# Time-step projection of a decoder trunk: normed x as the standing operand, 16 weight columns as the moving one

## The chip, the core and the metric

The kernel runs on one core of one Trainium2 chip. The metric is the device time of one execution in microseconds (us), the median of several runs. In all that follows PE is TensorE, PEld its weight loads (the loading of the operand that stands in the array), ACT is ScalarE, DVE is VectorE, POOL is GpSimd, and SP is the engine whose queue issues the DMAs.

## What is computed

The reference is one step of a two-layer decoder trunk over 1024 prompt tokens and 8 sample tokens. The change touches layer 0 alone, in the Mamba-2 part, where a raw time step for each of 16 heads is projected out of the normed x:

```
hn = _rmsnorm(x, norm_even[k])
proj = jnp.einsum('bld,de->ble', hn, w_in_even[k])
z, xbc, dt_raw, u, v, g = jnp.split(proj, EVEN_SPLITS, axis=-1)
...
dt = jax.nn.softplus(dt_raw.astype(jnp.float32) + dt_bias.astype(jnp.float32))
a = -jnp.exp(a_log.astype(jnp.float32))
...
da = jnp.transpose((dt * a).reshape(bsz, nc, T, G, E), (0, 1, 3, 4, 2))
cs = jnp.cumsum(da, axis=-1)
```

`dt_raw` has 16 of the 5648 columns of the projection. All other columns, the scan, the gates, the layer 1 and the outputs are the same in both kernels.

## The kernel before

The 1032 tokens (`NT`) lie along the free axis in nearly all of the kernel, and 128 features on the partitions. `hnh` and `hnl` hold the normed x as a high and a low part in float32r, 8 blocks (`k`) of 128 features by 1032 tokens. `unit` computes 128 output columns: it loads a weight block, splits it into high and low (`wh` by ACT at line 103, `wl` by DVE at line 104), and for each of three chunks of 344 tokens runs 8 blocks of three matmuls (lines 115 to 117): weights stand, x passes.

At the start, x comes in tokens on the partitions. For each of nine token blocks, `x_norm` norms a block, PE turns it (tiles `xnT`, line 220, two groups of four transposes, one in the bank pair `sA` and one in `sB`), ACT casts a group to `hnh` (line 223), and DVE takes the rest to `hnl` (line 224), which frees the bank. Each of `sA` and `sB` has two banks, so the second group of block 8 can be written when DVE has done the second group of block 6. While that goes on, PE works on the first two units, `B0` and `C0` (`mm_B`, `mm_C`), chunk by chunk as the tokens come, and on transposes of the parameters (`pct`, line 284).

`dt_unit` (line 376 of the kernel before) then makes the time steps. It loads 16 weight columns and splits them into a tile `wh_dt` of 128 x 8 x 32 (16 high columns beside 16 low ones), runs 3 chunks x 8 blocks x 2 matmuls with these columns standing and 344 tokens passing (lines 388 and 389), and ACT copies the 32 x 1032 result to `draw` (line 390). Ten small matmuls against a selecting matrix `sel` (lines 397 and 400) turn it to tokens on the partitions and add the two halves. Then DVE and ACT run `softplus` on 128 x 144 values, `dA` is formed with `ea` (the exponential of `ear`, 16 values loaded to all partitions by a DMA of its own, line 394), and PE makes the running sums (`cs`, `csT`, lines 408 to 419), which go to DRAM for the scan of the heads.

Every engine works its queue in order. The order is set at build time by a scheduler that walks the program with priorities (earlier in the program text goes first among what it takes to be ready), so that a statement that stands earlier in the text can land earlier in an engine's queue. A tile of a pool waits for the readers of the buffer's former tile; `ear` and `draw` are of the pool tag `mt` that also held the normed blocks `xn`. All DMAs are issued by SP in one queue.

Of the kernel before, what the change touches and what calls it, by code (L numbers as in the profile page):

```python
# [8 lines left out]
F32 = mybir.dt.float32  # L9
# [4 lines left out]
P = 128  # L14
L = 1024
NS = 8
NT = L + NS
CH = NT // 3
NB = 8
# [25 lines left out]
def tile_trunk(ctx, tc, a, o):  # L45
    nc = tc.nc
    V, S, T, G, SY = nc.vector, nc.scalar, nc.tensor, nc.gpsimd, nc.sync

    cp = ctx.enter_context(tc.tile_pool(name="cp", bufs=1))
# [6 lines left out]
    def blk(tag, name, shape=None, dt=F32):  # L56
        return hp.tile(shape or [P, NT], dt, name=name, tag=tag, bufs=NTAG[tag])

    def bank(tag, name):
        return pp.tile([P, 512], F32, name=name, tag=tag, bufs=4 if tag == "mm" else 2)  # L60
# [7 lines left out]
    def rowb(src, off, n, parts=P):  # L68
        return bass.AP(tensor=src.tensor, offset=src.offset + off, ap=[[0, parts], [1, n]])

    def tok(c):
        return (P, c * P) if c < 8 else (NS, L)

    ident = cp.tile([P, P], F32, name="ident")
# [16 lines left out]
    hn = [(hnh[:, k, :], hnl[:, k, :]) for k in range(NB)]  # L91
# [97 lines left out]
    for c in range(9):  # L189
        n = P if c < 8 else NS  # L190
# [161 lines left out]
    csv = cp.tile([P, 128], F32, name="csv")  # L352
    dec = cp.tile([P, 128], F32, name="dec")
    dtot = cp.tile([P, 128], F32, name="dtot")
    sel = cp.tile([32, 16], F32, name="sel")
    dtb = cp.tile([P, 16], F32, name="dtb")
    ea = cp.tile([P, 16], F32, name="ea")
    csd = dram("csd", [8, 16, P])
# [1 line left out]
    def softplus(dst, t, n, name):  # L360
        tm = blk("ld", "spt_" + name, [P, 4, n])
        e, s, s2, p = (tm[:, i, :] for i in range(4))
        V.scalar_tensor_tensor(e, t, -1.0, t, op0=OP.mult, op1=OP.max)
        S.activation(e, e, AF.Exp, scale=-1.0)
        V.tensor_scalar(s, e, 2.0, None, op0=OP.add)
        V.reciprocal(s, s)
        V.tensor_mul(s, s, e)
        V.tensor_mul(s2, s, s)
        V.tensor_scalar(p, s2, 1.0 / 15.0, None, op0=OP.mult)
        for q in (13.0, 11.0, 9.0, 7.0, 5.0, 3.0):  # L370
            V.scalar_tensor_tensor(p, p, 1.0 / q, s2, op0=OP.add, op1=OP.mult)
        V.scalar_tensor_tensor(p, p, 1.0, s, op0=OP.add, op1=OP.mult)
        V.tensor_scalar(e, t, 0.0, None, op0=OP.max)
        V.scalar_tensor_tensor(dst, p, 2.0, e, op0=OP.mult, op1=OP.add)

    def dt_unit():
        draw = blk("mt", "draw", [32, NT])
        with tc.high_priority(WPRI):
            raw = wp.tile([P, NB, 16], F32, name="wr_dt", tag="wr")
            SY.dma_start(raw, w_in_e[:, DTC:DTC + 16].rearrange("(k p) c -> p k c", p=P))  # L380
            whl = wp.tile([P, NB, 32], F32R, name="wh_dt", tag="wh")
            S.copy(whl[:, :, :16], raw)
            V.tensor_sub(whl[:, :, 16:], raw, whl[:, :, :16].bitcast(F32))
        for c in range(3):
            ps = bank("mm", f"mm_dt{c}")
            cs = slice(c * CH, (c + 1) * CH)
            for k, (xh, xl) in enumerate(hn):
                T.matmul(ps[:32, :CH], whl[:, k, :], xh[:, cs], start=k == 0, stop=False)
                T.matmul(ps[:16, :CH], whl[:, k, :16], xl[:, cs], start=False, stop=k == NB - 1)
            S.copy(draw[:, cs], ps[:32, :CH])  # L390
        V.tensor_add(sel, ident[:32, :16], ident[:32, 16:32])
        SY.dma_start(dtb, rowb(a["ssd_dt_bias"], 0, 16))
        ear = blk("mt", "ear", [P, 16])
        SY.dma_start(ear, rowb(a["ssd_a_log"], 0, 16))
        S.activation(ea, ear, AF.Exp)
        ps = bank("sA", "dtT")
        T.matmul(ps[:, 128:144], draw[:, :P], sel, start=True, stop=True)
        for c in range(9):
            n, lo = tok(c)
            T.matmul(ps[:n, c * 16:(c + 1) * 16], draw[:, lo:lo + n], sel, start=True, stop=True)  # L400
        dtr = blk("ld", "dtr", [P, 144])
        V.tensor_add(dtr.rearrange("p (c h) -> p c h", h=16), ps[:, :144].rearrange("p (c h) -> p c h", h=16),
                     dtb[:, None, :].to_broadcast([P, 9, 16]))
        softplus(dt, dtr, 144, "dt")
        V.scalar_tensor_tensor(dA.rearrange("p (c h) -> p c h", h=16), dt[:, :128].rearrange("p (c h) -> p c h", h=16),
                               -1.0, ea[:, None, :].to_broadcast([P, 8, 16]), op0=OP.mult, op1=OP.mult)
        ps = bank("sA", "cs")
        T.matmul(ps[:, :128], tri, dA, start=True, stop=True)
        T.matmul(ps[:, 128:256], ones, dA, start=True, stop=True)
        V.tensor_copy(csv, ps[:, :128])  # L410
        V.tensor_sub(dec, ps[:, 128:256], csv)
        S.activation(dec, dec, AF.Exp)
        S.activation(dtot, ps[:, 128:256], AF.Exp)
        csT = blk("ld", "csT", [16, 8, P])
        for q in range(2):
            ps = bank("sA", f"csT{q}")
            for i in range(4):
                c = q * 4 + i
                T.matmul(ps[:16, i * P:(i + 1) * P], dA[:, c * 16:(c + 1) * 16], tri, start=True, stop=True)
            S.copy(csT[:, q * 4:q * 4 + 4, :], ps[:16].rearrange("p (i t) -> p i t", i=4))  # L420
        SY.dma_start(csd.rearrange("c h l -> h c l"), csT)
# [205 lines left out]
    def g_unit(g, u, vl):  # L627
# [14 lines left out]
        SY.dma_start(mbd[g], u)  # L642

    dt_unit()
    for j in range(4):
        xj(j)
# [435 lines left out]
```

## Time and profile before

| | |
|---|---|
| median of 3 runs | 1498.07 us (1497.86 to 1498.74) |
| the profiled execution's own time | 1496.82 us |
| its span, first to last instruction | 1495.1 us |
| mean granted TensorE clock | 0.998 |
| busy: PE, PEld, DVE, ACT | 99%, 96%, 72%, 49% |
| DMA | 161.5 MB, 108 GB/s over the span |

Busy shares are over the whole span. Matmuls overlap in the records, each one's duration reaching over the start of the next, so the pace of a run of matmuls is read from one start to the next, not from the durations.

### The profile page before, as it was taken

The numbers are of one execution on the slowest core, as the hardware profiler recorded it, in microseconds if no ns is written. First come the engines' busy times: TensorE is split into PE (matmuls) and PEld (weight loads), VectorE is DVE, ScalarE is ACT, GpSimd is POOL, SyncE is SP. The second block draws the span as 40 slices with busy tenths as digits, with TensorE's granted clock in tenths as the row PEclk, the third lists the DMA queues.
The fourth block names the chain that finished last, engine by engine and source line by source line (L and its number), as shares of the span: only waits on it lengthen the run. The fifth ranks groups of instructions, "written<-read, shape, count | busy, mean of one in ns | idle before, by whom it ended". The sixth has DMA issues, their size and how long they took to land.

```text
span 1495.1 us, 23709 instructions
## 1 busy us (share of the span) xinstructions
PE 1476.4 (99%) x9850; PEld 1441.9 (96%) x9850; DVE 1077.1 (72%) x1493; ACT 727.0 (49%) x1094; POOL 0.9 (0%) x7
## 2 busy tenths in 40 slices
PE   7999999999999999999999999999999999999997
PEld 6899999999999999999999999999999999999997
DVE  6525676577777873663346799999999999869624
ACT  6457667585753242630224455465546663234313
POOL 0000000000000000000000000000000000000000
PEclk9999999999999999999999999999999999999999
DMA  6225322233325661236432113222222114357502
GB/s 202 71 74 146 110 85 83 61 124 114 102 96 176 213 198 43 91 120 215 141 113 95 51 33 104 75 61 68 64 76 61 43 58 128 100 188 236 158 29 114
DMA packets 179746, 161.52 MB, mean 108 GB/s; under 512 B 11176, under 2 KB 159324, under 8 KB 179606
## 3 DMA queue, kind: packets, MB, share of 16 engines
q1 hardware_dynamic: 179638, 160.01, 34.1%
q8 instruction: 77, 1.26, 0.4%
q14 instruction: 31, 0.25, 0.1%
HBM read 118.91 MB, written 42.18 MB: 108 GB/s over the span
## 4 chain that ended last, share of the span: by engine, by line
PE 91%; DVE 5%; ACT 2%; issue 1%; DMA 0%; SPq 0%; ACTq 0%; DVEq 0%
PE mm_x L115 2%; PE mm_x L117 2%; PE mm_gc L115 2%; PE mm_oa L115 2%; PE mm_ob L115 2%; PE mm_x L116 2%; PE mm_oa L117 2%; PE mm_oa L116 2%; PE mm_u L115 2%; PE mm_g L115 2%; PE mm_ob L117 2%; PE mm_gc L117 2%; PE mm_ob L116 2%; PE mm_u L117 2%; PE mm_g L116 2%; PE mm_g L117 2%
## 5 line engine op out<-in xcount | busy, mean ns | idle before, releaser
L894 DVE SCALAR_TENSOR_TENSOR c<-gl,pc,c 128x1023 f32<-128x1023 f32 (+25 forms) x240 | 294.9, 1260 | 1.1
L115 PE MATMUL mm_xd<-hnh,wh_xd 128*128 128x344 f32 x192 | 62.1, 323 | 0.7 <-ACT wh_xd L103 0.7
L115 PE MATMUL mm_u<-hnh,wh_u 128*128 128x344 f32 x192 | 62.7, 326 | 0.0
L117 PE MATMUL mm_v<-hnh,wl_v 128*128 128x344 f32 x192 | 62.4, 325 | 0.0
L116 PE MATMUL mm_v<-hnl,wh_v 128*128 128x344 f32 x192 | 62.3, 325 | 0.0
L115 PE MATMUL mm_ga<-hnh,wh_ga 128*128 128x344 f32 x192 | 62.2, 324 | 0.0
L115 PE MATMUL mm_v<-hnh,wh_v 128*128 128x344 f32 x192 | 62.2, 324 | 0.0
L117 PE MATMUL mm_x<-hnh,wl_x 128*128 128x344 f32 x192 | 62.1, 324 | 0.0
L117 PE MATMUL mm_gd<-hnh,wl_gd 128*128 128x344 f32 x192 | 62.0, 323 | 0.0
L115 PE MATMUL mm_gd<-hnh,wh_gd 128*128 128x344 f32 x192 | 62.0, 323 | 0.0
L115 PE MATMUL mm_z<-hnh,wh_z 128*128 128x344 f32 x192 | 61.6, 321 | 0.2 <-ACT sz L131 0.2
L115 PE MATMUL mm_x<-hnh,wh_x 128*128 128x344 f32 x192 | 61.8, 322 | 0.0
L116 PE MATMUL mm_u<-hnl,wh_u 128*128 128x344 f32 x192 | 61.7, 321 | 0.0
L115 PE MATMUL mm_g<-hnh,wh_g 128*128 128x344 f32 x192 | 61.7, 321 | 0.0
L116 PE MATMUL mm_g<-hnl,wh_g 128*128 128x344 f32 x192 | 61.7, 321 | 0.0
L116 PE MATMUL mm_x<-hnl,wh_x 128*128 128x344 f32 x192 | 61.7, 321 | 0.0
L115 PE MATMUL mm_gc<-hnh,wh_gc 128*128 128x344 f32 x192 | 61.6, 321 | 0.0
L117 PE MATMUL mm_u<-hnh,wl_u 128*128 128x344 f32 x192 | 61.6, 321 | 0.0
L115 PE MATMUL mm_gb<-hnh,wh_gb 128*128 128x344 f32 x192 | 61.5, 320 | 0.0
L117 PE MATMUL mm_g<-hnh,wl_g 128*128 128x344 f32 x192 | 61.4, 320 | 0.0
L116 PE MATMUL mm_gc<-hnl,wh_gc 128*128 128x344 f32 x192 | 61.4, 320 | 0.0
L116 PE MATMUL mm_gb<-hnl,wh_gb 128*128 128x344 f32 x192 | 61.4, 320 | 0.0
(477 smaller groups left out, 4927.8 us busy)
## 6 DMA issues: line engine op xcount, KB each, us to landing
x<-res SPq DMA_DIRECT2D x16, 516.0 KB
csb<-csd SPq DMA_DIRECT2D x16, 512.0 KB
mbd<-u SPq DMA_DIRECT2D x8, 516.0 KB
mbl<-mbd SPq DMA_DIRECT2D x8, 516.0 KB
rb<-res SPq DMA_DIRECT2D x8, 516.0 KB
res<-rb SPq DMA_DIRECT2D x8, 516.0 KB
res<-x SPq DMA_DIRECT2D x8, 516.0 KB
mdd<-hv SPq DMA_DIRECT2D x8, 516.0 KB
```

The costliest lines, as they stand in the source:

```text
L115: T.matmul(out, wh[:, k, :], xh[:, cs], start=i == 0, stop=False)
L116: T.matmul(out, wh[:, k, :], xl[:, cs], start=False, stop=False)
L117: T.matmul(out, wl[:, k, :], xh[:, cs], start=False, stop=i == NB - 1)
L894: V.scalar_tensor_tensor(c[:, d:L], gl[:, :L - d], w(k), c[:, d:L], op0=OP.mult, op1=OP.add)
```

## The change

The normed x now stands in the array, 128 tokens at a time, and the weight columns pass: for each of 9 token blocks (8 of 128 tokens and one of 8) 8 blocks of features x 2 matmuls, one that passes the 32 columns of `wh_dt` and one that passes 16, all into one bank `mm_dt`, 32 columns for each token block. The result has tokens on the partitions at once, so `draw`, its three copies, `sel` and the ten small matmuls go. DVE adds the bias and the second half in four operations rather than one. In the program text the DMAs of `dtb` and `ear` and the exponential of `ear` now stand ahead of the matmuls rather than behind them; `softplus` and all behind it are unchanged.

```diff
-    sel = cp.tile([32, 16], F32, name="sel")
...
     def dt_unit():
-        draw = blk("mt", "draw", [32, NT])
         with tc.high_priority(WPRI):
             raw = wp.tile([P, NB, 16], F32, name="wr_dt", tag="wr")
             SY.dma_start(raw, w_in_e[:, DTC:DTC + 16].rearrange("(k p) c -> p k c", p=P))
             whl = wp.tile([P, NB, 32], F32R, name="wh_dt", tag="wh")
             S.copy(whl[:, :, :16], raw)
             V.tensor_sub(whl[:, :, 16:], raw, whl[:, :, :16].bitcast(F32))
-        for c in range(3):
-            ps = bank("mm", f"mm_dt{c}")
-            cs = slice(c * CH, (c + 1) * CH)
-            for k, (xh, xl) in enumerate(hn):
-                T.matmul(ps[:32, :CH], whl[:, k, :], xh[:, cs], start=k == 0, stop=False)
-                T.matmul(ps[:16, :CH], whl[:, k, :16], xl[:, cs], start=False, stop=k == NB - 1)
-            S.copy(draw[:, cs], ps[:32, :CH])
-        V.tensor_add(sel, ident[:32, :16], ident[:32, 16:32])
         SY.dma_start(dtb, rowb(a["ssd_dt_bias"], 0, 16))
         ear = blk("mt", "ear", [P, 16])
         SY.dma_start(ear, rowb(a["ssd_a_log"], 0, 16))
         S.activation(ea, ear, AF.Exp)
-        ps = bank("sA", "dtT")
-        T.matmul(ps[:, 128:144], draw[:, :P], sel, start=True, stop=True)
+
+        ps = bank("mm", "mm_dt")
         for c in range(9):
             n, lo = tok(c)
-            T.matmul(ps[:n, c * 16:(c + 1) * 16], draw[:, lo:lo + n], sel, start=True, stop=True)
+            o0 = c * 32
+            for k, (xh, xl) in enumerate(hn):
+                T.matmul(ps[:n, o0:o0 + 32], xh[:, lo:lo + n], whl[:, k, :], start=k == 0, stop=False)
+                T.matmul(ps[:n, o0:o0 + 16], xl[:, lo:lo + n], whl[:, k, :16], start=False, stop=k == NB - 1)
         dtr = blk("ld", "dtr", [P, 144])
-        V.tensor_add(dtr.rearrange("p (c h) -> p c h", h=16), ps[:, :144].rearrange("p (c h) -> p c h", h=16),
-                     dtb[:, None, :].to_broadcast([P, 9, 16]))
+        d3 = dtr.rearrange("p (c h) -> p c h", h=16)
+        p3 = ps[:, :288].rearrange("p (c h) -> p c h", h=32)
+        V.memset(dtr[:, 128:], 0.0)
+        for n, cs in ((P, slice(0, 8)), (NS, slice(8, 9))):
+            V.tensor_add(d3[:n, cs], p3[:n, cs, :16], dtb[:n, None, :].to_broadcast([n, cs.stop - cs.start, 16]))
+            V.tensor_add(d3[:n, cs], d3[:n, cs], p3[:n, cs, 16:])
         softplus(dt, dtr, 144, "dt")
```

The built order of the instructions differs between the two kernels only from the casts of block 6 to the second of the `x` units (and in two neighbouring matmuls of the last pass). Three places matter. The first is ACT's queue behind the evacuation of `mm_C`'s first chunk, where the casts of blocks 6 to 8 stand (`xnT_265` and `xnT_272` are the two groups of block 6, `285` and `292` of block 7, `305` and `312` of block 8). Before:

```order
L136 COPY rw_C_123<-mm_C_0_403 128x344
L223 CAST hnh<-xnT_265 128x4x128
L223 CAST hnh<-xnT_272 128x4x128
L223 CAST hnh<-xnT_285 128x4x128
L223 CAST hnh<-xnT_292 128x4x128
L223 CAST hnh<-xnT_305 128x4x8
L223 CAST hnh<-xnT_312 128x4x8
L136 COPY rw_B_122<-mm_B_1_429 128x344
```

And now:

```order
L136 COPY rw_C_123<-mm_C_0_403 128x344
L223 CAST hnh<-xnT_265 128x4x128
L385 ACT_TABLE_LOAD
L385 ACTIVATE ea<-ear 128x16
L223 CAST hnh<-xnT_272 128x4x128
L223 CAST hnh<-xnT_285 128x4x128
L223 CAST hnh<-xnT_292 128x4x128
L223 CAST hnh<-xnT_305 128x4x8
L223 CAST hnh<-xnT_312 128x4x8
L136 COPY rw_B_122<-mm_B_1_429 128x344
```

The exponential of `ear` moved from behind the evacuation of the first `mm_dt` chunk to the middle of block 6, ahead of five of the casts.

The second is SP's queue of DMAs, in which three copies from DRAM to DRAM (old states to outputs) stand ahead of the next weight block. Before:

```order
L392 DMA dtb<-in_ssd_dt_bias_dram 128x16
L611 DMA w_578<-in_gmlp_w_s_dram 128x8x1
L679 DMA out_dram<-in_state_ssd_conv_dram 8x3072
L680 DMA out_dram<-in_state_ccv_dram 8x2x14848
L681 DMA out_dram<-in_state_lru_conv_dram 8x2048
L96 DMA wr_x_800<-in_w_in_even_dram 128x8x128
L295 DMA out_dram<-rows_B_543 3x128
L295 DMA out_dram<-rows_B_543 8x128
L394 DMA ear<-in_ssd_a_log_dram 128x16
```

And now:

```order
L382 DMA dtb<-in_ssd_dt_bias_dram 128x16
L608 DMA w_577<-in_gmlp_w_s_dram 128x8x1
L676 DMA out_dram<-in_state_ssd_conv_dram 8x3072
L677 DMA out_dram<-in_state_ccv_dram 8x2x14848
L678 DMA out_dram<-in_state_lru_conv_dram 8x2048
L384 DMA ear<-in_ssd_a_log_dram 128x16
L96 DMA wr_x_881<-in_w_in_even_dram 128x8x128
L295 DMA out_dram<-rows_B_543 3x128
```

The DMA of `ear` moved up past the weight block and the two stores of `rows_B`, and stands right behind the three copies.

The third is PE's queue from the end of `mm_C` on. Before (the 48 matmuls of `mm_dt` are shown by their first and last pairs):

```order
L289 MATMUL tl_B_541<-ident,rw_B_122 11x128
L388 MATMUL mm_dt_587<-hnh,wh_dt 32x344
L389 MATMUL mm_dt_587<-hnl,wh_dt 16x344
...
L388 MATMUL mm_dt_623<-hnh,wh_dt 32x344
L389 MATMUL mm_dt_623<-hnl,wh_dt 16x344
L397 MATMUL dtT<-sel,draw 128x16
L400 MATMUL dtT<-sel,draw 128x16 x2
L115 MATMUL mm_x_0_706<-hnh,wh_x_702 128x344
L400 MATMUL dtT<-sel,draw 128x16 x3
L116 MATMUL mm_x_0_706<-hnl,wh_x_702 128x344
```

And now (144 matmuls, 128 with 128 tokens standing and the last 16 with 8):

```order
L289 MATMUL tl_B_541<-ident,rw_B_122 11x128
L392 MATMUL mm_dt<-wh_dt,hnh 128x32
L393 MATMUL mm_dt<-wh_dt,hnl 128x16
...
L392 MATMUL mm_dt<-wh_dt,hnh 8x32
L393 MATMUL mm_dt<-wh_dt,hnl 8x16
```

The small matmuls are gone, three of which stood a chunk further down among those of `mm_x`, and the running sums (`cs`, `csT`) stand 56 matmuls behind the last `mm_dt`, earlier in the `x` units than before.

## Rows read from the trace of the kernel before

**Rows 1.** The page: busy time by engine, and the chain that ended last.

```profile
PE 1476.4 (99%) x9850; PEld 1441.9 (96%) x9850; DVE 1077.1 (72%) x1493; ACT 727.0 (49%) x1094; POOL 0.9 (0%) x7
...
PE 91%; DVE 5%; ACT 2%; issue 1%; DMA 0%; SPq 0%; ACTq 0%; DVEq 0%
```

**Rows 2.** Timeline of PE, 49 to 64: start, us, line, operation, tiles, form, count.

```profile
49.24 0.40 PE L388 MATMUL mm_dt<-hnh,wh_dt 128*32 128x344 f32 x1
...
57.84 0.43 PE L115 MATMUL mm_x<-hnh,wh_x 128*128 128x344 f32 x1
...
58.96 0.43 PE L116 MATMUL mm_x<-hnl,wh_x 128*128 128x344 f32 x1
59.22 0.32 PE L117 MATMUL mm_x<-hnh,wl_x 128*128 128x344 f32 x1
...
62.07 0.32 PE L117 MATMUL mm_x<-hnh,wl_x 128*128 128x344 f32 x1
...
63.22 0.42 PE L115 MATMUL mm_x<-hnh,wh_x 128*128 128x344 f32 x1
```

**Rows 3.** Timelines of the weight loads: `dtT` at 58, `mx` at 358.

```profile
58.19 0.74 PEld L400 LDWEIGHTS dtT<-sel,draw 32*128 32x128 f32 x6 [0.17 <-issue]
...
357.97 1.91 PEld L635 LDWEIGHTS mx<-wsT,vl 128*128 128x128 f32 x16
```

**Rows 4.** Timeline of PE in the last pass, float32r, 256 columns passing.

```profile
1484.10 0.28 PE L115 MATMUL mm_oc<-hnh,wh_oc 128*128 128x256 f32 x1
...
1484.92 0.28 PE L116 MATMUL mm_oc<-hnl,wh_oc 128*128 128x256 f32 x1
```

**Rows 5.** Timeline of ACT: casts of blocks 6 and 7 (first group), and `ea`.

```profile
30.03 1.79 ACT L223 CAST hnh<-xnT 128x512 fp32r<-128x512 f32 x3
...
54.32 0.22 ACT L395 ACTIVATE ea<-ear 128x16 f32<-128x16 f32 x1 [1.84 <-DMA ear<-in_ssd_a_log_dram]
```

**Rows 6.** Timeline of SP, DMA issues: start, us, line, transfer.

```profile
34.79 0.69 SPq L680 DMA_DIRECT2D out_dram<-in_state_ccv_dram  x1
35.53 0.68 SPq L681 DMA_DIRECT2D out_dram<-in_state_lru_conv_dram  x1
...
51.55 0.37 SPq L394 DMA_DIRECT2D ear<-in_ssd_a_log_dram  x1
```

**Rows 7.** Stretches of 0.5 us: engines' busy time, PEclk, DMA share, GB/s.

```profile
40.50:41.00 0.50, 0.50 (x6) 0.44 (x5) 0.23 (x1) 0.48 (x2) 0.00 (x0) 1.00 1.65 713
...
42.50:43.00 0.50, 0.50 (x6) 0.50 (x5) 0.00 (x0) 0.00 (x0) 0.00 (x0) 1.00 0.47 164
```

**Rows 8.** Timeline of DVE, the rests of blocks 6 and 7.

```profile
31.80 1.87 DVE L224 TENSOR_TENSOR hnl<-xnT,hnh 128x512 fp32r<-128x512 f32 x3
```

**Rows 9.** Timeline of PE, transposes of the second group of block 8.

```profile
36.54 0.41 PE L220 MATMUL xnT<-ident,xn 8*128 8x8 f32 x4
```

**Rows 10.** Timeline of PE at the start, and at the end of its work.

```profile
13.51 1.94 PE L220 MATMUL xnT<-ident,xn 128*128 128x128 f32 x8 [0.71 <-DVE xn L215]
...
17.99 0.49 PE L117 MATMUL mm_B<-hnh,wl_B 128*128 128x344 f32 x1
...
21.43 0.47 PE L117 MATMUL mm_C<-hnh,wl_C 128*128 128x344 f32 x1
21.72 0.34 PE L115 MATMUL mm_C<-hnh,wh_C 128*128 128x344 f32 x1
...
1486.47 0.28 PE L117 MATMUL mm_oc<-h_mc,wl_oc 128*128 128x256 f32 x1
...
1487.27 0.44 PE L1009 MATMUL fT<-ident,x 128*128 128x128 f32 x2 [0.30 <-DVE x L753]
```

**Rows 11.** Stretch of 2 us at the end, columns as in rows 7.

```profile
1488.00:1490.00 2.00, 0.00 (x0) 0.00 (x0) 1.10 (x4) 1.96 (x7) 0.00 (x0) 0.87 0.00 0
```

**Rows 12.** Timeline of DVE, from `dtr` to `dA`.

```profile
63.32 0.31 DVE L402 TENSOR_TENSOR dtr<-dtT,dtb 128x144 f32<-128x144 f32 x1 [3.73 <-PE dtT L400]
...
71.19 0.29 DVE L405 SCALAR_TENSOR_TENSOR dA<-dt,ea 128x128 f32<-128x128 f32 x1
```

## The prediction

> **What bounds the kernel now.** I read the page first: PE is busy for 99% of the span and carries 91% of the chain that ended last [rows 1]. So what PE spends on the path counts one for one, and time that another engine saves counts for nothing unless PE waits for it. Then I read the timelines around the change, 26 to 82 us, for what PE, ACT, DVE and SP do there, and compared them with the order of instructions in both builds. The places outside it keep their order, so a shift made here should be carried to the end.
>
> **The swapped matmuls.** What goes: from the first matmul of `mm_dt` at 49.24 to the first of `mm_x` at 57.84 there are 8.60 us; the small matmuls hold up `mm_x` twice more, 58.96 - 57.84 = 1.12 and 63.22 - 62.07 = 1.15 us where a step between two matmuls is 0.158 (59.22 to 62.07 in 18 steps), so 0.96 and 0.99 [rows 2]. Together 10.55, less some 0.2 for the one transpose `tl_C` that lies within and stays: 10.35 us go.
>
> What comes: 128 matmuls with 128 tokens standing and 16 with 8. No row before has this form in float32r. The nearest is `dtT` itself, 128 columns loaded and 16 passing: six loads span 0.74 us, the last of them 0.187 long, so a load starts every 0.111 us; sixteen loads of `mx` span 1.91 us, 0.115 a step [rows 3]. In float32r the last pass shows a 128-column load with 256 columns passing every 0.117 (0.82 us in 7 steps) [rows 4], about what 256 columns cost alone. The passing columns are thus too few to matter, and the load sets the pace: 128 x 0.112 = 14.3, and 1 us for the last 16 (between 0 and 1.8): 15.3 us at the full clock, 4.95 more than what goes. The bounds of the pace from these rows are 0.111 and 0.117, so 4.8 to 5.6.
>
> A rule with another price: the Trainium skill (TensorE: Matmul & The Clock Gate, section Back-to-back issue gap) gives some 81 ns for a pair of weight load and matmul with 128 columns passing. By it the 144 would take an estimated 11.7 us and the swap would cost 1.3, not 4.95; the rows with the same loads show 0.111 to 0.117, so I keep the rows.
>
> **The clock in that stretch.** At the start the same 344-column matmul steps 0.287 us (17.99 to 21.43 in 12 steps) and then 0.158: 344 columns at 1.2 GHz are 0.287, so PE ran at the lower level until about 21.7 [rows 10]. It rose once, 3.7 us into the first unbroken run of wide matmuls. The groups of short transposes ahead of that, such as the eight at 13.51, each a load with 128 columns passing, did not raise it. At the end it fell at 1489.5 (0.87 granted over 1488 to 1490) [rows 11], 2.9 us after the last wide matmul, though four transposes still ran between [rows 10]. The new stretch is 15 us of loads with 16 or 32 columns passing, less like the wide matmuls than those transposes were. I therefore take it that the clock falls within it. The stretches of this sort in the kernel before that I found are too short to tell (`mx`, 1.91 us [rows 3]), and so this is the weakest step.
>
> At the lower level a load steps 0.21 (eight transposes in 1.94 us, a tail like the 0.49 of a matmul there taken off, in 7 steps) [rows 10]. If the clock falls 4 us in, 36 matmuls are done by then; 92 x 0.21 = 19.3, the last 16 about 1.6, sum 24.9. The wide matmuls behind it start low and, with 3.7 us to the rise as at the start, lose 3.7 x (1 - 0.158/0.287) = 1.7. So 26.6 come where 10.35 go: +16.3 us. A fall 2 us earlier or later moves that by 1.7.
>
> **The moved exponential.** This part is not in the words of the change. With `draw` gone and the statements in another order, ACT's `ea` stands behind the first cast of block 6 and ahead of the five casts that follow. That first cast ends at about 30.6 (three in 1.79 us from 30.03) [rows 5]. SP reaches the DMA of `ear` when it has issued the three copies, 35.53 + 0.68 = 36.2 [rows 6], so ACT stands still for at least 5.6 us. When does `ear` land? The large copy of old states, issued at 34.79, shows as bursts of packets, the last at 40.5 to 41.0 with 713 GB/s, and the 64 KB copy issued behind it at 35.53 shows at 42.5 to 43.0 (0.5 us at 164 GB/s are 82 KB), seven us after its issue [rows 6, 7]. It waited behind the large copy. `ear` is issued right behind both, and I take it to land at 43.7, with the nearest alternative 36.2 + 2.8 = 39.0, as it took alone (51.55 to 54.32) [rows 5, 6].
>
> Whether its 128 rows go through the DMA engines that hold the copy no row shows. The Trainium skill (DMA: Bandwidth & Descriptors, section Why a DMA increments its semaphore by 16 and not by 1) says that a copy is spread over the largest number of engines, at most 16, that divides the slowest dimension of both sides, the lowest-numbered ones: 8 for the copies, 16 for `ear`. By that, half of `ear` lies behind the copy, and the late landing holds.
>
> What is queued behind `ea`: the cast of block 6's second group, 43.9 to 44.5, for which DVE's rest waits (0.62 each) [rows 8], done at about 45.2. That frees the bank that PE's transposes of block 8's second group need, which started at 36.54 [rows 9]. PE is in order: `pct` and the remaining matmuls of `mm_B` and `mm_C`, which need no cast, stand behind. So PE stops for 45.2 - 36.54 = 8.65 us. The casts that follow run ahead of PE, so nothing further is late. After such a pause the clock is low, by the fall at the end. The eight transposes there at 0.21 to 0.24 instead of 0.11 cost 0.9, and 3.7 us of wide matmuls cost 1.7: 2.6 us. Sum of this part +11.25; if `ear` lands at 39.0, PE waits until 40.5, 4.0 us, with up to 2.6 for the clock.
>
> **At nothing.** The three copies to `draw` were ACT's, off the path. DVE has three more small operations in the chain from `dtr` to `dA`, which took 8.2 us from 63.32 to 71.48 [rows 12]; ACT now loads the table for that exponential ahead of time, while DVE has a weight split of 1.2 us in between, so I count about 8.3. PE reaches `cs` 56 matmuls behind `mm_dt`, 8.8 us at the full clock and more at the lower one. That cover is thin: without it PE would wait for some tenths. The earlier running sums bring the scan's DMA forward, for which PE does not wait.
>
> **Sum.** 16.3 + 8.65 + 2.6 = 27.55 us. On the profiled execution's own 1496.82 that is 1524.4. The median of the runs is 1.25 above that execution, so 1525.6, rounded to 1526.
>
> **Rivals.**
> - The clock holds through the thin loads. For it: they leave PE no pause, and busy shares there will read full. Against: rows 10 and 11. Then 4.95 + 11.25 = 16.2 us come, and the time is 1514.3.
> - `ear` lands early, at 39.0, the copy's packets and its own not sharing engines. For it: no row shows that they share. Against: the 64 KB copy waited. Then 4.0 to 6.6 plus 16.3 or 4.95: 1518 to 1521 with the fall, 1507 to 1510 without.
> - Not slower: loads hide behind each other and the passing columns set the pace. The place is `mm_dt`; with 24 columns on average and the 0.014 us that a 344-column matmul takes over its 344/2.4 GHz, 0.024 x 144 = 3.5 us come, a gain of 6.9. It decides if the wait for `ear` costs less than that, so if `ear` lands before 41.9; at 39.0 the time is 1495.2. Against: rows 3 and 4, in which no 128-column load steps under 0.111.
>
> **How the numbers follow.** The forecast, both the fall and the late landing, gets 0.50, with an own range of 1522 to 1530 (fall 2 us earlier or later, landing 0.5 us, a rise after up to 5.7 us). The held clock gets 0.28, the early landing 0.15 in both its forms, the gain 0.04, and 0.03 stays for what I have not seen. The range 1511 to 1530 takes in the forecast, the held clock and the early landing with the fall, and leaves out about 0.18. Within 0.2% (3 us) a measurement of this kernel can't tell from no change. Only the gain ends there or below: faster 0.03, same 0.02, slower 0.95.
>
> **What would show it.** ACT idle for some 13 us ahead of `ea`, released by the DMA of `ear`; PE idle for 8 to 9 us from 36.6, released by DVE's `hnl`. In `mm_dt`, loads of 128 columns that step 0.11 at first and 0.21 later, a mean granted clock below 0.998, and 344-column matmuls at 0.49 for some us behind both places. Behind that, every line as before. The prediction is wrong if the `mm_dt` stretch lasts 15 us with the clock at 1.0, if `ea` runs before 40, or if a later wait takes up part of the shift.

## The result, and the profile after

The changed kernel takes 1524.47 us (median of 6 runs, 1523.13 to 1525.25), the kernel before 1498.07 (6 runs, 1497.56 to 1498.74): a ratio of 1.0177, 95% interval 1.0167 to 1.0188, so 26.4 us slower. The forecast was 1526, its range 1511 to 1530. The profiled execution took 1524.11 with a span of 1522.3, at a mean granted clock of 0.988.

The page answers to [rows 1]: PE's busy share and its share of the chain fell a point each.

```profile
PE 1494.2 (98%) x9926; PEld 1462.8 (96%) x9926; DVE 1077.3 (71%) x1496; ACT 725.7 (48%) x1091; POOL 0.9 (0%) x7
...
PE 90%; DVE 5%; ACT 2%; DMA 1%; issue 1%; SPq 0%; ACTq 0%; DVEq 0%
```

What a page averages away stands in the stretch from 36 to 93 us, in steps of 3 us (stretch, length, then busy time and count of PE, PEld, DVE, ACT and POOL, PEclk, DMA share, GB/s):

```profile
36.00:39.00 3.00, 1.38 (x10) 0.91 (x8) 0.00 (x0) 0.00 (x0) 0.00 (x0) 1.00 0.75 193
39.00:42.00 3.00, 0.00 (x0) 0.00 (x0) 0.00 (x0) 0.00 (x0) 0.00 (x0) 0.76 0.37 159
42.00:45.00 3.00, 0.00 (x0) 0.00 (x0) 0.01 (x1) 0.73 (x3) 0.00 (x0) 0.50 0.07 23
...
51.00:54.00 3.00, 3.00 (x23) 2.73 (x23) 1.12 (x4) 0.66 (x2) 0.00 (x0) 1.00 0.01 3
...
63.00:66.00 3.00, 3.00 (x23) 3.00 (x23) 3.00 (x5) 2.87 (x4) 0.00 (x0) 0.74 0.57 162
66.00:69.00 3.00, 3.00 (x15) 3.00 (x16) 2.18 (x3) 0.73 (x1) 0.00 (x0) 0.50 0.06 17
...
87.00:90.00 3.00, 3.00 (x17) 3.00 (x16) 2.54 (x7) 0.87 (x2) 0.00 (x0) 0.78 0.33 83
```

The clock falls twice, in two different situations. From 39 until ACT starts again at 44.27 no engine works at all, only DMAs move, and the clock falls at 40.5. From 66 on, PE and PEld read 3.00 of 3.00, fully busy, and the clock is at 0.50 all the same: here a full row of busy time says nothing about the clock. Only the counts (15 matmuls in 3 us) show how little is done.

The timelines of SP, ACT and PE show the first place (start, us, line, operation; in brackets the idle time ahead and what ended it). They answer to [rows 5, 6, 9].

```profile
35.36 0.70 SPq L677 DMA_DIRECT2D out_dram<-in_state_ccv_dram  x1
...
36.89 0.37 SPq L384 DMA_DIRECT2D ear<-in_ssd_a_log_dram  x1
```

```profile
31.44 1.28 ACT L385 ACT_TABLE_LOAD   x1
44.27 0.21 ACT L385 ACTIVATE ea<-ear 128x16 f32<-128x16 f32 x1 [11.55 <-DMA ear<-in_ssd_a_log_dram]
44.39 1.63 ACT L223 CAST hnh<-xnT 128x512 fp32r<-128x512 f32 x4
```

```profile
23.20 0.45 PE L117 MATMUL mm_C<-hnh,wl_C 128*128 128x344 f32 x1
23.48 0.32 PE L115 MATMUL mm_C<-hnh,wh_C 128*128 128x344 f32 x1
...
36.62 0.41 PE L220 MATMUL xnT<-ident,xn 8*128 8x8 f32 x4
36.96 0.42 PE L115 MATMUL mm_B<-hnh,wh_B 128*128 128x344 f32 x1
45.73 0.59 PE L220 MATMUL xnT<-ident,xn 8*128 8x8 f32 x4 [8.35 <-DVE hnl L224]
...
50.55 0.43 PE L115 MATMUL mm_C<-hnh,wh_C 128*128 128x344 f32 x1
50.82 0.32 PE L116 MATMUL mm_C<-hnl,wh_C 128*128 128x344 f32 x1
...
60.64 0.27 PE L289 MATMUL tl_B<-ident,rw_B 128*11 128x128 f32 x1
```

`ear` is issued at 36.89 and is used at 44.27, 7.4 us later. Four casts run as soon as it is there, DVE frees the bank, and PE, which had stood for 8.35 us, goes on at the lower level, 344 columns in 0.287 us, until 50.8. The first two rows are of the first rise of the clock: it came at about 23.4 in this execution and at 21.7 in that of before [rows 10], which brings PE to this place 0.77 us later (36.62, in the kernel before 35.85). That adds nothing behind the pause, because PE waits for `ear` whenever it arrives: in the e2 run below, with the same order there, PE is at the place at 35.67, stands for 9.36 us and goes on at 45.79, here at 45.73. So the pause costs 45.73 - 36.54 = 9.2 us against the kernel before [rows 9].

The loads of `mm_dt` show the second place. The answering rows are [rows 3], and for `tl_B`, the last matmul ahead of `mm_dt`, this one of the kernel before:

```profile
49.22 0.27 PE L289 MATMUL tl_B<-ident,rw_B 128*11 128x128 f32 x1
```

```profile
60.64 0.19 PEld L392 LDWEIGHTS mm_dt<-wh_dt,hnh 128*128 128x128 f32 x1
...
64.35 0.24 PEld L393 LDWEIGHTS mm_dt<-wh_dt,hnl 128*128 128x128 f32 x1
64.47 0.34 PEld L392 LDWEIGHTS mm_dt<-wh_dt,hnh 128*128 128x128 f32 x1
64.69 0.33 PEld L393 LDWEIGHTS mm_dt<-wh_dt,hnl 128*128 128x128 f32 x1
...
84.31 0.33 PEld L393 LDWEIGHTS mm_dt<-wh_dt,hnl 128*128 128x128 f32 x1
84.53 0.13 PEld L392 LDWEIGHTS mm_dt<-wh_dt,hnh 128*8 128x8 f32 x1
...
84.97 0.09 PEld L393 LDWEIGHTS mm_dt<-wh_dt,hnl 128*8 128x8 f32 x1
84.99 0.29 PEld L115 LDWEIGHTS mm_x<-hnh,wh_x 128*128 128x128 f32 x1
```

From 60.64 to 64.35 stand 33 steps of 0.112, from 64.69 to 84.31 92 steps of 0.2133: the clock fell 3.7 us into the thin stretch, with PE at work without a break since 45.73. The load of 128 columns, which set the pace, takes 1.9 times as long at the lower level. The 16 short loads take 0.46 us in all. The wide matmuls behind it stay at the lower level until 88.3.

Behind that next to nothing is taken back. The first of the scan's transposes, in both kernels (duration, first and last start, forms):

```profile
L436 PE MATMUL px<-ident,x x64: 270/272/329, 145.5 to 436.5; 128*128 128x128 f32 x64
```

```profile
L433 PE MATMUL px<-ident,x x64: 269/272/329, 173.0 to 464.0; 128*128 128x128 f32 x64
```

Both first and last are 27.5 us later; the spans differ by 27.2. About 1 us of the 27.5 is a new wait: the transposes `xT` of line 235 are still 26.5 us later at 162.07 (135.56 before), and at 163.79 PE stands 0.81 us for ACT's `xo`, which it does not do at that place in the kernel before.

### The profile page after: what moved, and what is told of

Same layout as the page of the kernel before. It is cut to its first block, busy times and chain, and to the rows that moved or that the text cites. A ratio compares the mean times of both kernels' runs of the same rounds, so it can differ in the third digit from the quotient of the medians.

```text
span 1522.3 us, 23860 instructions
## 1 busy us (share of the span) xinstructions
PE 1494.2 (98%) x9926; PEld 1462.8 (96%) x9926; DVE 1077.3 (71%) x1496; ACT 725.7 (48%) x1091; POOL 0.9 (0%) x7
## 4 chain that ended last, share of the span: by engine, by line
PE 90%; DVE 5%; ACT 2%; DMA 1%; issue 1%; SPq 0%; ACTq 0%; DVEq 0%
PE mm_x L115 2%; PE mm_x L117 2%; PE mm_x L116 2%; PE mm_gc L115 2%; PE mm_oa L115 2%; PE mm_ob L117 2%; PE mm_oa L116 2%; PE mm_oa L117 2%; PE mm_u L115 2%; PE mm_ob L116 2%; PE mm_g L115 2%; PE mm_u L117 2%; PE mm_g L117 2%; PE mm_ob L115 2%; PE mm_gc L117 2%; PE mm_v L117 2%
## 5 line engine op out<-in xcount | busy, mean ns | idle before, releaser
L117 PE MATMUL mm_gb<-hnh,wl_gb 128*128 128x344 f32 x192 | 61.5, 320 | 0.0
L117 PE MATMUL mm_z<-hnh,wl_z 128*128 128x344 f32 x192 | 61.4, 320 | 0.0
```

The source lines that it names most:

```text
L117: T.matmul(out, wl[:, k, :], xh[:, cs], start=False, stop=i == NB - 1)
```

## Experiments

The theory: two separate costs, the wait of ACT for `ear` (some 11 us) and the thin loads, which cost 4 to 5 us by their pace and some 11 by the clock, which falls while only 16 or 32 columns pass. The rivals: the clock fell only because of the pause ahead; the loads make it fall whatever passes; `ear` was held by something else than the copy; the exponential costs time by its place. Times below are against the kernel before in the same series (1497.71, 1498.07 and 1498.06 us).

**e1, the move undone.** The run is the changed kernel in which a buffer is held as `draw` held it, and the DMA and the exponential stand behind the matmuls again. The buffer is needed: with the text alone put back, the scheduler places the exponential ahead of the casts all the same, since without `draw` a buffer of that tag is free for `ear`.

```diff
+        draw = blk("mt", "draw", [32, NT])
...
-        ear = blk("mt", "ear", [P, 16])
-        SY.dma_start(ear, rowb(a["ssd_a_log"], 0, 16))
-        S.activation(ea, ear, AF.Exp)
...
+        S.copy(draw[:, :32], ps[:32, :32])
+        ear = blk("mt", "ear", [P, 16])
+        SY.dma_start(ear, rowb(a["ssd_a_log"], 0, 16))
+        S.activation(ea, ear, AF.Exp)
```

> The changed kernel with the move alone undone: the DMA and the exponential of the 16 values stand behind the matmuls again, in the text and on ACT, by a buffer held as `draw` held it; the swapped matmuls stay. My theory, that the thin loads let the clock fall by themselves: the matmuls cost 24.4 us in place of 10.35 as in the changed kernel, and about 1.5 us go until the clock is back, so 15.5 us over the kernel before, 1513.5 (1512 to 1515); loads step 0.111 for some 4 us and then 0.213. Rival, that the clock fell there only because the pause of 8 us came ahead of it: loads step 0.111 throughout, the granted clock is 0.998, and the time is 4 to 6 us over the kernel before, 1503.

1513.31 us, ratio 1.0104 (1.0089 to 1.0119): +15.6. PE has no wait from 26 to 49 us, and the clock falls all the same, 3.1 us after the first thin matmul at 49.17:

```profile
52.18 0.27 PE L389 MATMUL mm_dt<-wh_dt,hnl 128*128 128x16 f32 x1
52.31 0.38 PE L388 MATMUL mm_dt<-wh_dt,hnh 128*128 128x32 f32 x1
52.52 0.36 PE L389 MATMUL mm_dt<-wh_dt,hnl 128*128 128x16 f32 x1
```

The rival falls.

**e2, the move alone,** in the kernel before.

```diff
-        draw = blk("mt", "draw", [32, NT])
...
+        SY.dma_start(dtb, rowb(a["ssd_dt_bias"], 0, 16))
+        ear = blk("mt", "ear", [P, 16])
+        SY.dma_start(ear, rowb(a["ssd_a_log"], 0, 16))
+        S.activation(ea, ear, AF.Exp)
+        draw = blk("mt", "draw", [32, NT])
         for c in range(3):
```

> The kernel before with the move alone: DMA and exponential of the 16 values ahead of the matmuls in the text, so that on ACT the exponential stands ahead of five casts; the projection as before. My theory, that the wait adds to the path in full: PE stops 8.3 us at 36.5, and some 2.5 us go at the lower clock behind it, so 11 us over the kernel before, 1509 (1507.5 to 1510.5). Rival, that later waits shrink and take part of the shift back: 0 to 8 us over the kernel before.

1508.48 us, ratio 1.0070 (1.0055 to 1.0085): +10.8. ACT's `ea` and PE's transposes of block 8:

```profile
44.32 0.22 ACT L386 ACTIVATE ea<-ear 128x16 f32<-128x16 f32 x1 [12.58 <-DMA ear<-in_ssd_a_log_dram]
```

```profile
35.67 0.41 PE L220 MATMUL xnT<-ident,xn 8*128 8x8 f32 x4
36.01 0.42 PE L115 MATMUL mm_B<-hnh,wh_B 128*128 128x344 f32 x1
45.79 0.59 PE L220 MATMUL xnT<-ident,xn 8*128 8x8 f32 x4 [9.36 <-DVE hnl L224]
```

The time is in the range of the first theory. The pause was taken as 8.3 us and is 9.36: PE came to the place earlier than in the changed kernel and went on at the same time. The shift is carried to the end, and 15.6 + 10.8 = 26.4 is what both parts cost together: they add up.

**e3, more columns behind the same loads,** on e1: each of the 128 full matmuls passes the 32 weight columns eight times over.

```diff
-                T.matmul(ps[:n, o0:o0 + 32], xh[:, lo:lo + n], whl[:, k, :], start=k == 0, stop=False)
-                T.matmul(ps[:n, o0:o0 + 16], xl[:, lo:lo + n], whl[:, k, :16], start=False, stop=k == NB - 1)
+            r = 8 if c < 8 else 1
...
+                w8 = whl[:, k, None, :].to_broadcast([P, r, 32])
+                d8 = ps[:n, o0:o0 + 32 * r]
+                T.matmul(d8, xh[:, lo:lo + n], w8, start=k == 0, stop=False)
+                T.matmul(d8, xl[:, lo:lo + n], w8, start=False, stop=k == NB - 1)
```

> The kernel of e1 with the same 128-column loads, but 256 columns passing in each of the 128 matmuls of the full blocks (the 32 weight columns eight times over), written to five banks. My theory, that the clock falls because so few columns pass: it stays at 1.0, loads step 0.117, 128 x 0.117 + 0.5 = 15.5 us in place of 10.35, so 5 us over the kernel before, 1503 (1502 to 1505). Rival, that the row of loads behind each other makes it fall, whatever passes: the clock is lower for most of the stretch, the step goes to 0.213, and the time is that of e1, 1512 to 1515.

1501.97 us, ratio 1.0026 (1.0016 to 1.0036): +4.3, in the range of the first theory. PEclk is 1.00 in each stretch of 3 us from 48 to 66, with 27 matmuls in most where e1 has 15, and the step is 0.121. The same stretch in e3 and then in e1:

```profile
54.00:57.00 3.00, 3.00 (x27) 3.00 (x26) 2.57 (x6) 1.94 (x3) 0.00 (x0) 1.00 0.09 20
```

```profile
54.00:57.00 3.00, 3.00 (x15) 3.00 (x16) 2.68 (x5) 0.63 (x3) 0.00 (x0) 0.50 0.26 75
```

Behind the same loads, 256 columns take 11.3 us less than 16 or 32. So the row of loads alone doesn't make the clock fall: with 16 or 32 columns passing it fell, with 256 it held. (e3 also writes five banks rather than one; no run separates that.)

**e4, without the large copy** ahead of `ear` (the copy of old ccv states is left out).

```diff
-    SY.dma_start(o["ccv_sample"][0, :, 0:29, :], a["state_ccv"][0, :, 1:30, :])
```

> The changed kernel without the large copy of old ccv states that SP issues just ahead of the DMA of `ear` (that output is left unwritten); the order on all engines is otherwise that of the changed kernel. My theory, that `ear` landed late because it stood behind that copy: it lands about 3 us after its issue, near 39, PE stops 3 to 4 us in place of 8.35, and the time is 4.5 to 7.5 us under the changed kernel, 1517 to 1520. Rival, that something else held it (the smaller copy, the weight block behind it, its own 128 small pieces): it still lands 7 us after its issue, near 43.5, and the time is within 1.5 us of the changed kernel, 1523 to 1525.

1518.37 us, ratio 1.0135 (1.0120 to 1.0150): +20.7, 5.7 less than the changed kernel's +26.4.

```profile
35.45 0.37 SPq L384 DMA_DIRECT2D ear<-in_ssd_a_log_dram  x1
```

```profile
38.31 0.21 ACT L385 ACTIVATE ea<-ear 128x16 f32<-128x16 f32 x1 [6.88 <-DMA ear<-in_ssd_a_log_dram]
```

```profile
39.78 0.59 PE L220 MATMUL xnT<-ident,xn 8*128 8x8 f32 x4 [3.70 <-DVE hnl L224]
```

`ear` is used 2.9 us after its issue rather than 7.4, with the smaller copy and its own 128 rows as before. The large copy ahead held it. Whether through shared DMA engines or otherwise no run shows.

**e5, thin matmuls spread out,** on e1's order: two behind each wide matmul of the second and third `x` unit, in the first two of their three chunks. The weight columns stand in the buffer that `draw` had.

```diff
+    def mix(c, i):
+        if thin and c != 2:
+            for _ in range(2):
+                next(thin[0], None)
...
             T.matmul(out, wh[:, k, :], xh[:, cs], start=i == 0, stop=False)
+            mix(c, 3 * i)
```

> The thin matmuls as in the changed kernel, the exponential behind them, but spread out: from the third chunk of the first `x` unit on, two thin ones behind each 344-column matmul of the next two units (first two chunks of each; the weight columns stand in a buffer of the tag that held `draw`). My theory: the wide matmuls hold the clock at 1.0, and each thin one still costs its load, 0.111, so 128 x 0.111 + 0.5 = 14.7 us in place of 10.35: 4 to 5 us over the kernel before, 1502. First rival, that the loads hide behind the columns of the wide matmuls: 0.02 to 0.06 for a thin one, 3 to 9 us in all, so 1 to 7 us under the kernel before, 1491 to 1496. Second rival, that the clock falls all the same, since two matmuls of three are thin: a step of 0.72 for a wide and two thin ones instead of 0.38, 20 us or more over the kernel before.

1502.18 us, ratio 1.0030 (1.0020 to 1.0040): +4.1, the first theory. The clock is at 1.00 throughout, and from one wide matmul to the next:

```profile
64.16 0.40 PE L124 MATMUL mm_x<-hnl,wh_x 128*128 128x344 f32 x1
64.40 0.18 PE L399 MATMUL mm_dt<-wh_dt,hnh 128*128 128x32 f32 x1
64.44 0.26 PE L401 MATMUL mm_dt<-wh_dt,hnl 128*128 128x16 f32 x1
64.55 0.40 PE L126 MATMUL mm_x<-hnh,wl_x 128*128 128x344 f32 x1
```

are 0.39 us. A wide one alone steps 0.158, so a thin one adds 0.116, about its load. A wide neighbour hides nothing of it.

**e6, thin matmuls in pieces,** as e5, but 24 at a time with at least 12 wide ones between.

```diff
-            for _ in range(2):
+            for _ in range(24 if i % 12 == 8 else 0):
```

> As e5, but in six pieces of 24 thin matmuls (2.7 us of loads at 0.111) with 12 wide matmuls (1.9 us) or more between two pieces. My theory, that the clock falls 3 to 4 us into an unbroken thin stretch and not earlier: it stays at 1.0, and the time is that of e5, 4 to 5 us over the kernel before, 1502. Rival, that the mean over a longer time counts, in which thin ones now take 60 per cent: the clock falls in some of the pieces, loads there step 0.213, and the time is 8 to 20 us over the kernel before.

1509.39 us, ratio 1.0079 (1.0062 to 1.0096): +11.3. The theory for this run falls. The first piece runs at the full clock to its end, and the clock falls 0.7 us behind it, among wide matmuls:

```profile
65.01 0.26 PE L401 MATMUL mm_dt<-wh_dt,hnl 128*128 128x16 f32 x1
65.12 0.41 PE L122 MATMUL mm_x<-hnh,wh_x 128*128 128x344 f32 x1
...
65.68 0.32 PE L122 MATMUL mm_x<-hnh,wh_x 128*128 128x344 f32 x1
65.84 0.43 PE L124 MATMUL mm_x<-hnl,wh_x 128*128 128x344 f32 x1
66.07 0.49 PE L126 MATMUL mm_x<-hnh,wl_x 128*128 128x344 f32 x1
```

It is back at 76.1, falls at 79.5, comes back at 82.9 in the middle of a thin piece, and falls once more at 86.4. So the theory had the place of the fall wrong: the clock ran full through 2.6 us of thin matmuls and came down behind them. Three of the six pieces were followed by a fall, one ran wholly at the lower level, and behind the last two the clock held. The sixth is short, 1.2 us, since 16 of its loads are of 8 columns; why the fifth differs stays open.

**e7, the data early,** in the changed kernel: `ear` has a buffer of its own and its DMA stands with the first parameters.

```diff
         SY.dma_start(hrow[1:2], a["ssd_a_log"])
+        SY.dma_start(ear, rowb(a["ssd_a_log"], 0, 16))
```

> The changed kernel with `ear` in a buffer of its own and its DMA issued with the first parameters, ahead of the copies of old states; the exponential stays ahead of the matmuls in the text (on ACT it lands at block 4, with one table load more to come back to the square root). My theory, that only the late data cost time there: ACT runs the exponential without a wait of microseconds, PE does not stop at block 8, and the time is that of e1, 15 to 17 us over the kernel before, 1513 to 1515. Rival, that an exponential among the casts costs PE time by itself, by the two table loads of 1.28 us and the casts behind them: 2 to 4 us more than e1, 1516 to 1518.

1513.66 us, ratio 1.0103 (1.0086 to 1.0120): +15.6, the same as e1. ACT no longer waits, and two table loads in the middle of the casts cost PE nothing that can be measured:

```profile
22.09 1.28 ACT L386 ACT_TABLE_LOAD   x1
23.39 0.22 ACT L386 ACTIVATE ea<-ear 128x16 f32<-128x16 f32 x1
23.62 1.28 ACT L213 ACT_TABLE_LOAD   x1
```

No run beats the kernel before: the best forms of the swap, e3 and e5, are 4 us behind it.

## Why the prediction was right

Term by term, from the profiled execution of the changed kernel against that of before:

| term | predicted | measured | from |
|---|---|---|---|
| pause of PE | 8.65 | 9.2 | 45.73 - 36.54 |
| lower clock behind it | 2.6 | 2.2 | `tl_B` 11.42 later (49.22 to 60.64), less 9.19 |
| the thin stretch | 24.9 | 24.4 | 60.64 to 85.02, first `mm_x` |
| what goes | -10.35 | -10.55 | [rows 2], with the place of `tl_C` in both |
| lower clock behind the thin stretch | 1.7 | 1.6 | 11 wide matmuls in 3.30 us from 85.02, less 11 x 0.158 |
| sum | 27.55 | 26.8 | |

The spans differ by 27.2, the medians by 26.4. The new wait for `xo` is about 1 us that the sum lacks, and 0.3 go again by the first `xT` and another 0.3 behind `px`; those are not assigned. No term is off by more than 0.6, and the misses partly cancel.

- **The pace of the loads** was taken from `dtT` and `mx` at 0.112, and came at 0.112. The Trainium skill (TensorE: Matmul & The Clock Gate, section Back-to-back issue gap) has some 81 ns for such a pair with 128 columns passing; no stretch of 128-column loads here goes under 0.11, and e5 shows 0.116 for a thin matmul also between wide ones. The same page's section on LDWEIGHTS has the loaded columns over 1.2 in ns, an estimated 107 ns for 128. The rows at the full clock come near that with 0.112; those at the lower level, with 0.2133, don't. The cost at the full clock, predicted as 4.95, is 4.3 in e3 and 4.1 in e5.
- **The fall of the clock,** the weakest step, held: 35 matmuls were done where 36 were taken, and each of the rest took 0.213. That the thin stretch itself brings it was shown afterwards by e1 (no pause needed) and e3 (with 256 columns it holds). The likeness to the end of the kernel was an argument only: there the clock falls at 1489.5, when PE has stood since 1487.7. That it falls 4 us in is in no row either; it came after 3.7 here and 3.1 in e1, so the closeness of the 36 is in part luck.
- **The rise of the clock** was taken 3.7 us into a run of wide matmuls, counted from 17.99. The run starts at 17.54, so it is 4.2 there. Behind the thin stretch it took 3.3 us, behind the pause 5.1, and 5.8 at the start of the changed kernel: the 3.7 is one value of several.
- **One size was far off for its term:** the last 16 matmuls. Their loads of 8 columns, priced at 1.6 us, took 0.46.
- **The moved exponential** went as followed along the queues: `ear` at 44.27 where 43.7 was taken, behind the copy (e4), and PE held by the bank that DVE frees. What the prediction left open, whether the text or the missing `draw` moved it, the built orders show: either is enough. What the prediction did not follow is the later wait for `xo`.
- **At nothing** was right. The chain from `dtr` at 85.20 to the end of `dA` at 93.3 took 8.1 us, and PE came to `cs` at 95.39.

```profile
85.20 0.29 DVE L399 TENSOR_TENSOR dtr<-mm_dt,dtb 128x128 f32<-128x128 f32 x1 [17.02 <-PE mm_dt L393]
...
92.99 0.29 DVE L402 SCALAR_TENSOR_TENSOR dA<-dt,ea 128x128 f32<-128x128 f32 x1
```

```profile
95.39 0.38 PE L405 MATMUL cs<-dA,tri 128*128 128x128 f32 x2
```

Of the rivals, "not slower" fell to the loads' pace, the held clock is what e3 and e5 make of the kernel, and the early landing what e4 makes of it: each at its place, none in the changed kernel.

## What to carry to other kernels

Here a matmul with 16 or 32 passing columns cost its weight load, 0.112 us for 128 columns. Before turning the operands round, weigh the loads that come against the columns that go: 128 such loads came here for 48 matmuls at 0.158 us and ten small ones. Look at the pace and the granted clock of such a stretch, not at its busy share: PE can be full and at half its clock. And when a tile goes, look at what else its buffer held back: here a 16-column exponential moved ahead of the casts and stopped PE for 8 us, and the order of the queues showed it before any run.

## What was not expected of the hardware

- The clock fell while wide matmuls ran, 0.7 us behind a thin piece that had itself run at full clock (e6, 65.84), and took until 76.1 to come back, with another thin piece in between.
- PEclk reads 1.00 from 22 to 24 us in both kernels, while the changed one steps 0.287 for 344 columns until 23.4 there. Ahead of the first change of the clock in a trace, its level is read from the step, not from that column.
- Loads of 8 columns step 0.026 us at the lower level (84.60 to 84.97 in 14 steps), about a quarter of a 128-column load at the full clock, and in e6 they step 0.026 at the full clock too (97.81 to 98.18 in 14 steps). So the short loads do not slow with the clock, where those of 128 columns do.
